# A hybrid decoder block: the FFN's weight sums made by accumulating DMAs, and its first block as eight plain products

## The chip, the cores and the metric

The kernel runs on one core of a Trainium2 chip. The metric is device microseconds of one execution. Profiles come from one profiled execution, and their times count from the first instruction of its span.

## The reference

One decoder block on 512 tokens of width 1024, in float32. Two mixers (a Mamba-2 scan and a gated delta rule) are merged, projected by `w_out` and added to `x`. Behind them stands the part that the change touches, a SwiGLU FFN with 2816 hidden columns:

```python
x = x + merged @ w_out[l]
h = rmsnorm(x, norm_ffn_w[l])
gate, up = jnp.split(h @ w_ffn_in[l], [FFN_HIDDEN], axis=-1)
x = x + (jax.nn.silu(gate) * up) @ w_ffn_down[l]
return rmsnorm(x, final_norm_w)
```

## The kernel before

Every large product is made in three matmuls of a rounded type: each operand is split into a high part (an ACT cast, `whi` for weights) and a low part (a DVE subtraction, `wlo`), and `three` (L322) adds high x high, high x low and low x high in PSUM.

**Order of the work.** The instruction order on TensorE, DVE and ACT is fixed when the program is built. A planner (`Weave`, L34) keeps an estimated clock for each engine; `job`s run one after the other and issue the products, and threads (evictions, norms, sums) are emitted between matmuls by `tick` (L85) when their events are done by that estimate. `until` (L104) moves the planned clock of TensorE on until an event is done. On the chip each engine goes through its own queue in order and waits on semaphores.

**Weights.** `stream` is the list of weight units in the order of use. A unit is 512 rows by 256 columns, 512 KB. `load` (L306) issues the DMA of the next unit on SP's queue, or calls a function that does and returns a tile; `ahead(n_split, n_load)` (L280) splits units ahead of the product in hand, and `ahead(2, 3)` stands in the middle of each product. `whi`, `wlo` and the load tile `wst` have three buffers each. Larger tiles share pools: `b8` (16 buffers), `m4` (5) and, for 512 elements a partition, `s2` (8). PSUM has eight banks (`psum`).

**The FFN input.** Tokens are halved (0 to 255, 256 to 511), and so are the 1024 input columns. With the gate and the up columns of one block of 256 hidden columns, this is a 2 x 2 product of 2 x 2 blocks: activations a11, a12 (first token half), a21, a22 (second), and weights b11, b21 (gate) and b12, b22 (up). Strassen's scheme, in Winograd's form, makes it in seven products instead of eight: P1 = a11 b11, P2 = a12 b21, and five products with sums on one side or on both. There are 11 blocks (`NB`). A product is two column groups of 128 times four row groups times three matmuls of 256 columns: 24 matmuls.

The activation sums are made once, by `h2_sums` (L1141): for token half 0 it splits a11 (P1) and a12 (P2), for half 1 a22 (P4) and then the sums for P5, P7, P6 and P3, each a DVE sum and a split. They wait for the norm and the transposes of the token tiles (`norm_T`, L382), whose two scalar steps run on GpSimd.

The weight sums are made for each block by GpSimd in `ffn_units` (L1247): t1 = b12 - b11, t2 = b22 - t1, b22 - b12 and b21 - t2, four tensor_tensor operations on 128 x 1024 elements. `ffn_post` (L1288) adds the products of a block and applies Silu and the gate, on ACT and DVE. `act_split` (L1364) splits the result for the down projection, which follows (`down_job`, L1377).

Of the kernel before, what the change touches and what calls it, by code (L numbers as in the profile page):

```python
# [8 lines left out]
F32 = mybir.dt.float32  # L9
F32R = mybir.dt.float32r  # L10
# [116 lines left out]
class Queue:  # L127
# [3 lines left out]
    def __getattr__(self, name):  # L131
        f = getattr(self.eng, name)
        wv = self.wv

        def emit(out_, *args, **kw):
            if name == "dma_start":
                wv.cur += 2500.0
                wv.last = None
            else:
                n = free_size(out_)  # L140
                if name == "reciprocal":
                    n *= 8
# [3 lines left out]
                if self.key == "POOL" and name == "tensor_tensor" and ALU.pow not in args:  # L146
                    cost = 200.0 + 2.1 * n
# [31 lines left out]
def hybrid_block_kernel(  # L179
# [21 lines left out]
    def nm(s):  # L201
        uid[0] += 1
        return f"{s}_{uid[0]}"
# [76 lines left out]
    def ahead(n_split, n_load):  # L280

        main = wv.cur
        for i in range(len(splits), min(at[0] + n_split, len(stream))):
            _, a, b = stream[i]
            while len(loads) <= i:
                load()
            wv.cur = max(wv.clock["PE"], loads[i][1])
            hi = wp.tile([P, a, b], F32R, tag="whi", name=nm("whi"))
            lo = wp.tile([P, a, b], F32R, tag="wlo", name=nm("wlo"))
            split(hi, lo, loads[i][0])  # L290
            splits.append((hi, lo, wv.cur))
            if len(loads) < min(i + 1 + n_load, len(stream)):
                load()
        while len(loads) < min(len(splits) + n_load, len(stream)):
            load()
        wv.cur = main

    def fetch(src, a, b, pool=None):
        if pool:
            st = pool([a, b], s="wst")  # L300
        else:
            st = wp.tile([P, a, b], F32, tag="wst", name=nm("wst"))
        sy.dma_start(st, src)
        return st

    def load():  # L306
        src, a, b = stream[len(loads)]
# [833 lines left out]
    def h2_sums(th):  # L1141


        (a11, a12) = mid.hq[0][:, 0], mid.hq[0][:, 1]
        if th == 0:
            yield [("h2", 0), ("h2", 1)]
            h2_split("P1", a11)
            yield HOP
            h2_split("P2", a12)
            return  # L1150
        (a21, a22) = mid.hq[1][:, 0], mid.hq[1][:, 1]
        yield [("h2", 2), ("h2", 3), ("a", "P2")]
        h2_split("P4", a22)
        s1 = m4([4, 256], s="s1")
        ve.tensor_tensor(s1, a21, a22, ALU.add)
        yield HOP
        h2_split("P5", s1)
        yield HOP
        ve.tensor_tensor(a21, a11, a21, ALU.subtract)
        h2_split("P7", a21)  # L1160
        yield HOP
        ve.tensor_tensor(a11, s1, a11, ALU.subtract)
        h2_split("P6", a11)
        yield HOP
        ve.tensor_tensor(a12, a12, a11, ALU.subtract)
        h2_split("P3", a12)

    def wo_job(q):
        if q == 0:
# [77 lines left out]
    def ffn_units(fp, order):  # L1247
        w = Batch()

        def get(r, c, pool=None):  # L1250
            return fetch(ffn_src(r, c, fp), 4, 256, pool)

        def t1():
            w.b11 = get(0, 0)
            w.b12 = get(0, 1, m4)
            w.t1 = b8([4, 256], F32, "t1")
            gp.tensor_tensor(w.t1, w.b12, w.b11, ALU.subtract)

        def t2():
            w.b22 = get(1, 1, m4)  # L1260
            w.t2 = m4([4, 256], s="t2")
            gp.tensor_tensor(w.t2, w.b22, w.t1, ALU.subtract)

        def of(name):
            if name == "P1":
                t1()
                return w.b11
            if name == "P6":
                if not hasattr(w, "t1"):
                    t1()  # L1270
                t2()
                return w.t2
            if name == "P7":
                gp.tensor_tensor(w.b12, w.b22, w.b12, ALU.subtract)
                return w.b12
            if name == "P5":
                w.b21 = get(1, 0)
                return w.t1
            if name == "P2":
                return w.b21  # L1280
            if name == "P4":
                gp.tensor_tensor(w.t2, w.b21, w.t2, ALU.subtract)
                return w.t2
            return w.b22

        return [((lambda n=n: of(n)), 4, 256) for n in order]

    def ffn_post(fp):  # L1288

        v = ffn.act[fp]  # L1290
        lo, hi = slice(0, 256), slice(256, 512)

        def half(s_):
            t = s2([512], s_)
            return t, t.rearrange("p (j t) -> p j t", j=2)

        bk = ffn.banks[fp]
        yield [("P", fp, "P1")]
# [6 lines left out]
        yield [("P", fp, "P7")]  # L1305
        u3, _ = half("u3")
        ve.tensor_tensor(u3, bk["C"], u2, ALU.add)
        yield [("P", fp, "P5")]
        c22, c22v = half("c22")
        ve.tensor_tensor(c22, bk["D"], u3, ALU.add)  # L1310
        finish(("c22", fp))
        yield [("P", fp, "P2")]
        ac.activation(v[:, :, lo], bk["A"].rearrange("p (j t) -> p j t", j=2), AF.Silu)
        yield [("P", fp, "P4")]
        ve.tensor_tensor(u3, bk["E"], u3, ALU.add)
        yield HOP
        ac.activation(v[:, :, hi], u3.rearrange("p (j t) -> p j t", j=2), AF.Silu)
        yield HOP
        ve.tensor_tensor(v[:, :, hi], c22v, v[:, :, hi], ALU.mult)
        yield [("P", fp, "P3")]  # L1320
        ve.tensor_tensor(u2, bk["D"], u2, ALU.add)
        ve.tensor_tensor(v[:, :, lo], u2.rearrange("p (j t) -> p j t", j=2), v[:, :, lo], ALU.mult)
        finish(("ffn", fp))
        yield True

    ffn.banks = {}

    def product(fp, name):

        if fp not in ffn.banks:  # L1330
            ffn.banks[fp] = {}
            if fp % 2 == 0:
                ffn.pair = b8([2, 2, T], F32, "act")
            ffn.act.append(ffn.pair[:, fp % 2])
            spawn(ffn_post(fp))
        until(("a", name), *{"P2": [("p1", fp)], "P3": [("c22", fp)]}.get(name, []))
        bk = ffn.banks[fp]
        fresh = BANK[name] not in bk
        if fresh:
            bk[BANK[name]] = psum("pw")  # L1340
        p = bk[BANK[name]]
        ahi, alo = ffn.a[name]
        whi, wlo = unit()
        for j in range(2):
            cs = slice(j * P, (j + 1) * P)
            for kk in range(4):
                three(p[:, 256 * j:256 * j + 256], (whi[:, kk, cs], wlo[:, kk, cs]), (ahi[:, kk], alo[:, kk]),
                      fresh and j == 0 and kk == 0, j == 1 and kk == 3, skip_group_check=True)
                if kk % 2:
                    tick()  # L1350
            if j == 0:
                ahead(2, 3)
        finish(("P", fp, name))

    def ffn_block(fp, order=ORDER):
        for name in order:
            product(fp, name)

    for fp in range(NB):
        job(lambda fp=fp: ffn_block(fp), *ffn_units(fp, ORDER))  # L1360

    act = {}

    def act_split():  # L1364

        for fp in range(NB):
            yield [("ffn", fp), ("P", NB - 1, "P5" if fp == 0 else ORDER[(fp + 1) // 2 - 1])]
# [118 lines left out]
```

## Time and profile before

| | us |
|---|---|
| median of three runs | 1045.8 (1044.96 to 1046.6) |
| the profiled execution | 1047.84 |
| its span, first to last instruction | 1046.1 |
| TensorE busy in the span | 998.0 |
| DVE, ACT, GpSimd (POOL) busy | 673.6, 457.6, 193.5 |

Matmuls overlap, so TensorE's busy time is longer than its work at full rate: read the starts. In a timeline row the bracket gives the idle time before the operation and who ended it. Line 155 is the helper through which DVE, ACT, GpSimd and SP operations go, line 166 the one of matmuls; go by the tiles' names. The granted clock is a share of TensorE's 2.4 GHz.

### The profile page before, as it was taken

The numbers are of one execution on the slowest core, as the hardware profiler recorded it, in microseconds if no ns is written. First come the engines' busy times: TensorE is split into PE (matmuls) and PEld (weight loads), VectorE is DVE, ScalarE is ACT, GpSimd is POOL, SyncE is SP. The second block draws the span as 40 slices with busy tenths as digits, with TensorE's granted clock in tenths as the row PEclk, the third lists the DMA queues.
The fourth block names the chain that finished last, engine by engine and source line by source line (L and its number), as shares of the span: only waits on it lengthen the run. The fifth ranks groups of instructions, "written<-read, shape, count | busy, mean of one in ns | idle before, by whom it ended". The sixth has DMA issues, their size and how long they took to land.

```text
span 1046.1 us, 15585 instructions
## 1 busy us (share of the span) xinstructions
PE 998.0 (95%) x6370; PEld 885.6 (85%) x6370; DVE 673.6 (64%) x901; ACT 457.6 (44%) x834; POOL 193.5 (18%) x148
## 2 busy tenths in 40 slices
PE   7999999999999999999999999398999999999997
PEld 5888878888888888788998899398999989988886
DVE  5665899545576867842255545578887888772422
ACT  5466445467867472022344323443334443552322
POOL 2041002100101210000011003344545555000000
PEclk9999999999999999999999999789999999999999
DMA  6242232121124533243223531222233322232222
GB/s 191 80 165 61 84 99 81 42 81 42 41 62 141 178 95 96 72 124 96 86 82 101 162 100 61 60 81 81 81 109 116 100 81 82 81 120 90 94 81 81
DMA packets 84072, 98.30 MB, mean 94 GB/s; under 512 B 5738, under 2 KB 75527, under 8 KB 83232
## 3 DMA queue, kind: packets, MB, share of 16 engines
q1 hardware_dynamic: 83998, 97.30, 30.3%
q8 instruction: 50, 0.82, 0.3%
q14 instruction: 22, 0.18, 0.1%
q10 hardware_dynamic: 2, 0.00, 0.0%
HBM read 95.14 MB, written 2.15 MB: 93 GB/s over the span
## 4 chain that ended last, share of the span: by engine, by line
PE 83%; DVE 11%; ACT 2%; issue 2%; SPq 1%; DMA 0%; POOL 0%; POOLq 0%; ACTq 0%; DVEq 0%
PE pw L166 52%; PE pdn L166 11%; PE pt L166 8%; DVE wlo L155 5%; PE pyd L166 1%; DVE act L155 1%; DVE gd L155 1%; PE pm L166 1%; DVE xb L155 1%; PE pt L170 1%; PE pn L170 1%; SPq L155 1%; PE pa L166 1%; PE po L166 1%; PE pg L166 1%
## 5 line engine op out<-in xcount | busy, mean ns | idle before, releaser
L155 DVE TENSOR_TENSOR wlo<-wst,whi 128x1024 fp32r<-128x1024 f32 x158 | 215.1, 1363 | 223.7 <-ACT whi L155 217.2
L155 ACT CAST whi<-wst 128x1024 fp32r<-128x1024 f32 x158 | 165.4, 1049 | 207.1 <-PE pw L166 114.4
L166 PE MATMUL pw<-h2w,whi 128*128 128x256 f32 x1232 | 225.3, 285 | 14.2 <-ACT h2w L155 12.2
L166 PEld LDWEIGHTS pw<-h2w,whi 128*128 128x128 f32 x1232 | 194.1, 194 | 14.7 <-ACT h2w L155 12.4
L166 PE MATMUL pw<-hhi,whi 128*128 128x512 f32 (+1 forms) x496 | 196.7, 397 | 1.4 <-ACT whi L155 1.4
L166 PE MATMUL pw<-hhi,wlo 128*128 128x512 f32 (+1 forms) x496 | 191.1, 385 | 2.3 <-DVE wlo L155 2.3
L166 PE MATMUL pw<-hlo,whi 128*128 128x512 f32 (+1 forms) x496 | 190.6, 384 | 0.0
L166 PE MATMUL pw<-h2w,wlo 128*128 128x256 f32 x616 | 177.2, 288 | 12.1 <-DVE wlo L155 12.1
L166 PEld LDWEIGHTS pw<-h2w,wlo 128*128 128x128 f32 x616 | 119.2, 194 | 15.5 <-DVE wlo L155 15.5
L166 PEld LDWEIGHTS pw<-hhi,wlo 128*128 128x128 f32 x496 | 93.7, 189 | 21.9 <-DVE wlo L155 3.0
L166 PEld LDWEIGHTS pw<-hhi,whi 128*128 128x128 f32 x496 | 93.8, 189 | 17.9 <-ACT whi L155 1.6
L166 PE MATMUL pdn<-whi,actw 128*128 128x512 f32 x352 | 108.4, 389 | 0.0
L166 PEld LDWEIGHTS pw<-hlo,whi 128*128 128x128 f32 x496 | 94.0, 190 | 16.3
L166 PEld LDWEIGHTS pdn<-whi,actw 128*128 128x128 f32 x352 | 66.1, 188 | 13.6
L155 POOL TENSOR_TENSOR t<-wst,t 128x1024 f32<-128x1024 f32 x22 | 61.9, 2814 | 49.7 <-DVE wlo L155 40.1
L166 PE MATMUL pdn<-wlo,actw 128*128 128x512 f32 x176 | 68.5, 389 | 0.0
L155 DVE TENSOR_TENSOR wlo<-t,whi 128x1024 fp32r<-128x1024 f32 x33 | 57.7, 1749 | 3.0 <-ACT whi L155 3.0
L155 POOL TENSOR_TENSOR t<-wst,wst 128x1024 f32<-128x1024 f32 x11 | 29.5, 2678 | 153.7 <-PE pt L166 75.7
L155 DVE SCALAR_TENSOR_TENSOR acc<-pw,pg,acc 128x511 f32<-128x511 f32 (+2 forms) x72 | 53.6, 747 | 2.8 <-ACT acc L155 0.9
L155 ACT CAST whi<-t 128x1024 fp32r<-128x1024 f32 x33 | 34.5, 1045 | 32.4 <-PE pw L166 32.4
L166 PE MATMUL pw<-yg,whi 128*128 128x512 f32 x128 | 42.9, 416 | 0.0
L155 POOL TENSOR_SCALAR ss<-ss 128x1 f32<-128x1 f32 x16 | 4.9, 304 | 196.4 <-ACT jk L155 179.2
(262 smaller groups left out, 1639.6 us busy)
## 6 DMA issues: line engine op xcount, KB each, us to landing
wst<-in_w_in_dram SPq DMA_DIRECT2D x68, 512.0 KB, 3.7
wst<-in_w_ffn_in_dram SPq DMA_DIRECT2D x44, 512.0 KB, 3.8
wst<-in_w_ffn_down_dram SPq DMA_DIRECT2D x22, 512.0 KB, 3.8
decay<-gcd SPq DMA_DIRECT2D x6, 1024.0 KB, 4.9
wst<-in_w_proj_gdn_dram SPq DMA_DIRECT2D x8, 512.0 KB, 3.5
wst<-in_w_proj_ssm_dram SPq DMA_DIRECT2D x8, 512.0 KB, 3.5
wst<-in_w_out_dram SPq DMA_DIRECT2D x8, 512.0 KB, 3.6
xt<-in_x_dram SPq DMA_DIRECT2D x4, 512.0 KB, 4.5
```

The lines of the kernel that those rows point to most:

```text
L155: return f(out_, *args, **kw)
L166: return self.eng.matmul(out_, lhsT, rhs, **kw)
L170: return self.eng.transpose(out_, in_, identity)
```

## The change

The change does four things.

1. The order of the products and the signs of the sums are others (`ORDER`, `BANK`). All weight sums are now additions: x is b11, then b11 + b12, then b11 + b12 + b22; y is b22, then b22 + b12; z is b21, then b21 + x. The two accumulations into x, the one into y and the one into z are DMAs with `accum_op=ALU.add`, issued on GpSimd's queue. Three of them read the weights from DRAM once more, the last reads x from SBUF.
2. A new class, `Source`, holds for a unit what loads it and what is to be done right after its split (`post`, called in `ahead`). So x is added to as soon as P1's split has read it, and the next product that uses x takes its split from the same tile.
3. Block 0 is made as eight plain products (`ffn_first`): the four of the first token half first, then the four of the second. Its four weight units are split once into `b8` tiles that stay (`keep`). `h2_sums` also splits a21 for it.
4. `ffn_post` evicts in another grouping: six DVE evictions and two gate products per block instead of five and two; block 0 has one Silu and one product for each half. The planner's cost for GpSimd's tensor_tensor is dropped.

```diff
@@ in ahead()
+            src = stream[i][0]
+            if getattr(src, "keep", False):
+                both = b8([2, a, b], F32R, "wkeep")
+                hi, lo = both[:, 0], both[:, 1]
+            else:
+                hi = wp.tile([P, a, b], F32R, tag="whi", name=nm("whi"))
+                lo = wp.tile([P, a, b], F32R, tag="wlo", name=nm("wlo"))
             split(hi, lo, loads[i][0])
+            if callable(src):
+                src.post()
@@ in h2_sums()
         yield [("h2", 2), ("h2", 3), ("a", "P2")]
+        h2_split("a21", a21)
+        yield HOP
         h2_split("P4", a22)
         s1 = m4([4, 256], s="s1")
-        ve.tensor_tensor(s1, a21, a22, ALU.add)
+        ve.tensor_tensor(s1, a21, a22, ALU.subtract)
         yield HOP
         h2_split("P5", s1)
-        yield HOP
         ve.tensor_tensor(a21, a11, a21, ALU.subtract)
+        yield HOP
+        ve.tensor_tensor(s1, s1, a11, ALU.subtract)
+        h2_split("P6", s1)
+        yield HOP
+        ve.tensor_tensor(a12, a12, s1, ALU.add)
+        h2_split("P3", a12)
+        yield HOP
         h2_split("P7", a21)
...
-    ORDER = ("P1", "P6", "P7", "P5", "P2", "P4", "P3")
-    BANK = {"P1": "A", "P6": "B", "P7": "C", "P5": "D", "P2": "A", "P4": "E", "P3": "D"}
+    ORDER = ("P1", "P3", "P2", "P5", "P7", "P6", "P4")
+    BANK = {"P1": "A", "P3": "F", "P2": "A", "P5": "D", "P7": "C", "P6": "B", "P4": "E"}
@@ ffn_units()
+        if fp == 0:
+            return [(Source(lambda r=r, c=c: fetch(ffn_src(r, c, 0), 4, 256), keep=True), 4, 256)
+                    for c in range(2) for r in range(2)]
...
+        def get(name, r, c, pool=None):
+            setattr(w, name, fetch(ffn_src(r, c, fp), 4, 256, pool))
+            return getattr(w, name)
+
+        def add(dst, src):
+            gp.dma_start(dst, src, accum_op=ALU.add)
+
+        def t2_t4():
+            add(w.x, ffn_src(1, 1, fp))
+            add(w.z, w.x)
+
+        return [(Source(g, p), 4, 256) for g, p in (
+            (lambda: get("x", 0, 0, m4), lambda: add(w.x, ffn_src(0, 1, fp))),
+            (lambda: get("y", 1, 1, m4), lambda: add(w.y, ffn_src(0, 1, fp))),
+            (lambda: get("z", 1, 0), None),
+            (lambda: w.x, t2_t4),
+            (lambda: w.y, None),
+            (lambda: w.x, None),
+            (lambda: w.z, None))]
@@ ffn_post(), a block that is not the first
+        yield [("P", fp, "P2")]
+        ac.activation(v[:, :, lo], two(bk["A"]), AF.Silu)
         yield [("P", fp, "P6")]
         u2, _ = half("u2")
+        u3, _ = half("u3")
         ve.tensor_tensor(u2, bk["B"], p1, ALU.add)
...
         ve.tensor_tensor(u3, bk["C"], u2, ALU.add)
+        ve.tensor_tensor(u2, bk["F"], u2, ALU.subtract)
+        ve.tensor_tensor(u2, bk["D"], u2, ALU.add)
+        ve.tensor_tensor(v[:, :, lo], two(u2), v[:, :, lo], ALU.mult)
...
+        ve.tensor_tensor(c22, bk["D"], u3, ALU.subtract)
@@ new
+    def ffn_first():
+
+        ffn_start(0)
+        ws = {}
+        for t, cs in ((1, (1, 2)), (2, (2, 1))):
+            for c in cs:
+                p = ffn.banks[0][f"c{t}{c}"] = psum("pw")
+                for r in (1, 2):
+                    name = {(1, 1): "P1", (1, 2): "P2", (2, 1): "a21", (2, 2): "P4"}[t, r]
+                    until(("a", name))
+                    if t == 1:
+                        ws[r, c] = unit()
+                    product(p, ffn.a[name], ws[r, c], r == 1, r == 2, lambda: ahead(2, 3))
+                finish(("P", 0, f"c{t}{c}"))
```

## Rows read from the trace of the kernel before

**Rows 1.** The page's first part: busy time, share of the span, instructions.
```profile
PE 998.0 (95%) x6370; PEld 885.6 (85%) x6370; DVE 673.6 (64%) x901; ACT 457.6 (44%) x834; POOL 193.5 (18%) x148
```

**Rows 2.** TensorE's timeline: an early FFN matmul, and every third of an undisturbed product.
```profile
655.83 0.40 PE L166 MATMUL pw<-h2w,whi 128*128 128x256 f32 x2
...
882.12 0.28 PE L166 MATMUL pw<-h2w,wlo 128*128 128x256 f32 x1
...
882.48 0.28 PE L166 MATMUL pw<-h2w,wlo 128*128 128x256 f32 x1
```

**Rows 3.** Busy time by stretch: length, engines with counts, granted clock, DMA share, GB/s.
```profile
core 0: us, PE busy (x) PEld busy (x) DVE busy (x) ACT busy (x) POOL busy (x), PEclk, DMA share, GB/s
655.80:701.50 45.70, 26.79 (x187) 26.08 (x186) 29.85 (x25) 19.34 (x24) 17.32 (x10) 0.78 0.20 60
730.70:752.57 21.87, 20.66 (x170) 20.26 (x169) 18.77 (x16) 8.84 (x11) 11.42 (x4) 1.00 0.33 97
...
701.50:919.70 218.20, 206.10 (x1683) 202.65 (x1682) 185.77 (x143) 91.89 (x105) 99.47 (x36) 1.00 0.30 92
```

**Rows 4.** TensorE's timeline, its gaps: start, length, operation, count, idle before and releaser.
```profile
639.57 0.39 PE L166 MATMUL pt<-wlo,mgh 128*128 128x256 f32 x1 [1.48 <-DVE wlo L155]
...
663.62 3.48 PE L170 MATMUL pt<-ident,hn 128*128 128x128 f32 x16 [4.75 <-DVE hn L155]
...
679.27 0.58 PE L166 MATMUL pw<-h2w,whi 128*128 128x256 f32 x1 [12.17 <-ACT h2w L155]
681.84 0.58 PE L166 MATMUL pw<-h2w,whi 128*128 128x256 f32 x1 [1.99 <-DVE h2w L155]
...
885.12 0.38 PE L166 MATMUL pw<-h2w,wlo 128*128 128x256 f32 x1 [1.04 <-DVE wlo L155]
```

**Rows 5.** Waits of TensorE, 701.5 to 919.7: total us, times, longest.
```profile
PE pw L166 <- DVE wlo L155: 12.1, 17, 1.5
```

**Rows 6.** The chain of waits in one block: start, length, engine, tile.
```profile
854.32 1.34 DVE act L155
855.66 3.36 DVE wlo L155
859.07 2.91 PE pw L166 x22
861.98 1.21 DVE wlo L155
863.23 11.55 PE pw L166 x94
```

**Rows 7.** Timelines of GpSimd and DVE in one block.
```profile
880.97 2.41 POOL L155 TENSOR_TENSOR t<-wst,t 128x1024 f32<-128x1024 f32 x1 [1.16 <-DVE wlo L155]
...
864.24 0.68 DVE L155 TENSOR_TENSOR u<-pw,p 128x512 f32<-128x512 f32 x1
...
881.53 2.40 DVE L155 TENSOR_TENSOR act<-u,act 128x512 f32<-128x512 f32 x1
```

**Rows 8.** Timelines of ACT and DVE in block 0.
```profile
660.52 1.03 ACT L155 CAST whi<-wst 128x1024 fp32r<-128x1024 f32 x1
...
667.76 1.04 ACT L155 CAST h2w<-hq 128x1024 fp32r<-128x1024 f32 x1
...
668.83 1.23 DVE L155 TENSOR_TENSOR h2w<-hq,h2w 128x1024 fp32r<-128x1024 f32 x1 [3.37 <-ACT h2w L155]
```

**Rows 9.** Timelines of ACT and DVE, one undisturbed split.
```profile
868.93 1.05 ACT L155 CAST whi<-wst 128x1024 fp32r<-128x1024 f32 x1 [1.78 <-PE pw L166]
...
870.01 1.23 DVE L155 TENSOR_TENSOR wlo<-wst,whi 128x1024 fp32r<-128x1024 f32 x1
```

**Rows 10.** DMA issues of the whole span: count, size of each, median us to landing.
```profile
decay<-gcd SPq DMA_DIRECT2D x6, 1024.0 KB, 4.9
wst<-in_w_proj_gdn_dram SPq DMA_DIRECT2D x8, 512.0 KB, 3.5
```

**Rows 11.** The same, 701.5 to 919.7.
```profile
wst<-in_w_ffn_in_dram SPq DMA_DIRECT2D x32, 512.0 KB, 4.2
```

More of the change, by code (lines that the diff above doesn't have):

```diff
@@ L145, in emit @@
                 cost = self.fixed + self.rate * n
-                if self.key == "POOL" and name == "tensor_tensor" and ALU.pow not in args:
-                    cost = 200.0 + 2.1 * n
                 if ALU.pow in args:
@@ L287, in ahead @@
             wv.cur = max(wv.clock["PE"], loads[i][1])
-            hi = wp.tile([P, a, b], F32R, tag="whi", name=nm("whi"))
-            lo = wp.tile([P, a, b], F32R, tag="wlo", name=nm("wlo"))
+            src = stream[i][0]
[5 more added lines that the diff above has]
+                lo = wp.tile([P, a, b], F32R, tag="wlo", name=nm("wlo"))
             split(hi, lo, loads[i][0])
+            if callable(src):
+                src.post()
             splits.append((hi, lo, wv.cur))
@@ L304, in fetch, with __init__, __call__, post @@
         return st
+    class Source:
+        def __init__(self, get, post=None, keep=False):
+            self.get, self.after, self.keep = get, post, keep
+        def __call__(self):
+            return self.get()
+        def post(self):
+            if self.after:
+                main, last = wv.cur, wv.last
+                self.after()
+                wv.cur, wv.last = main, last
     def load():
@@ L1152, in h2_sums @@
         yield [("h2", 2), ("h2", 3), ("a", "P2")]
+        h2_split("a21", a21)
+        yield HOP
         h2_split("P4", a22)
         s1 = m4([4, 256], s="s1")
-        ve.tensor_tensor(s1, a21, a22, ALU.add)
+        ve.tensor_tensor(s1, a21, a22, ALU.subtract)
         yield HOP
         h2_split("P5", s1)
+        ve.tensor_tensor(a21, a11, a21, ALU.subtract)
         yield HOP
-        ve.tensor_tensor(a21, a11, a21, ALU.subtract)
-        h2_split("P7", a21)
-        yield HOP
[L1162 to L1166, printed above, removed]
+        ve.tensor_tensor(s1, s1, a11, ALU.subtract)
[4 more added lines that the diff above has]
+        yield HOP
+        h2_split("P7", a21)
     def wo_job(q):
@@ L1245, in ffn_src, with ffn_units @@
         return w_ffn_in[512 * r:512 * r + 512, off:off + 256].rearrange("(k p) c -> p k c", p=P)
-    def ffn_units(fp, order):
+    def ffn_units(fp):
+        if fp == 0:
+            return [(Source(lambda r=r, c=c: fetch(ffn_src(r, c, 0), 4, 256), keep=True), 4, 256)
+                    for c in range(2) for r in range(2)]
         w = Batch()
[L1250 to L1286, printed above, removed]
+        def get(name, r, c, pool=None):
[14 more added lines that the diff above has]
+            (lambda: w.z, None))]
     def ffn_post(fp):
@@ L1297, in ffn_post, with two @@
         bk = ffn.banks[fp]
+        def two(t):
+            return t.rearrange("p (j t) -> p j t", j=2)
+        if fp == 0:
+            for name, s_ in (("c11", lo), ("c21", hi)):
+                yield [("P", fp, name)]
+                ac.activation(v[:, :, s_], two(bk[name]), AF.Silu)
+                yield [("P", fp, name[:2] + "2")]
+                ve.tensor_tensor(v[:, :, s_], two(bk[name[:2] + "2"]), v[:, :, s_], ALU.mult)
+            finish(("ffn", fp))
+            yield True
+            return
         yield [("P", fp, "P1")]
@@ L1316, in ffn_post @@
         yield HOP
-        ac.activation(v[:, :, hi], u3.rearrange("p (j t) -> p j t", j=2), AF.Silu)
+        ac.activation(v[:, :, hi], two(u3), AF.Silu)
         yield HOP
         ve.tensor_tensor(v[:, :, hi], c22v, v[:, :, hi], ALU.mult)
-        yield [("P", fp, "P3")]
-        ve.tensor_tensor(u2, bk["D"], u2, ALU.add)
-        ve.tensor_tensor(v[:, :, lo], u2.rearrange("p (j t) -> p j t", j=2), v[:, :, lo], ALU.mult)
         finish(("ffn", fp))
@@ L1326, in hybrid_block_kernel, with ffn_start, product @@
     ffn.banks = {}
[L1328 to L1343, printed above, removed]
+    def ffn_start(fp):
+        ffn.banks[fp] = {}
+        if fp % 2 == 0:
+            ffn.pair = b8([2, 2, T], F32, "act")
+        ffn.act.append(ffn.pair[:, fp % 2])
+        spawn(ffn_post(fp))
+    def product(p, a, w, first, last, each=None):
         for j in range(2):
@@ L1346, in product, with ffn_block @@
             for kk in range(4):
-                three(p[:, 256 * j:256 * j + 256], (whi[:, kk, cs], wlo[:, kk, cs]), (ahi[:, kk], alo[:, kk]),
-                      fresh and j == 0 and kk == 0, j == 1 and kk == 3, skip_group_check=True)
+                three(p[:, 256 * j:256 * j + 256], (w[0][:, kk, cs], w[1][:, kk, cs]), (a[0][:, kk], a[1][:, kk]),
+                      first and j == 0 and kk == 0, last and j == 1 and kk == 3, skip_group_check=True)
                 if kk % 2:
                     tick()
[L1351 to L1357, printed above, removed]
+            if j == 0 and each:
+                each()
+    def ffn_first():
[11 more added lines that the diff above has]
+                finish(("P", 0, f"c{t}{c}"))
+    def ffn_block(fp):
+        ffn_start(fp)
+        bk = ffn.banks[fp]
+        for name in ORDER:
+            until(("a", name), *([("p1", fp)] if name == "P2" else []))
+            fresh = BANK[name] not in bk
+            if fresh:
+                bk[BANK[name]] = psum("pw")
+            w = unit()
+            product(bk[BANK[name]], ffn.a[name], w, fresh, True, lambda: ahead(2, 3))
+            finish(("P", fp, name))
     for fp in range(NB):
-        job(lambda fp=fp: ffn_block(fp), *ffn_units(fp, ORDER))
+        job(lambda fp=fp: ffn_block(fp) if fp else ffn_first(), *ffn_units(fp))
     act = {}
@@ L1366, in act_split @@
         for fp in range(NB):
-            yield [("ffn", fp), ("P", NB - 1, "P5" if fp == 0 else ORDER[(fp + 1) // 2 - 1])]
+            yield [("ffn", fp), ("P", NB - 1, ORDER[max(0, (fp + 1) // 2 - 1)])]
             w = b8([2, 2, T], F32R, "actw")
```

7 lines of the change are left out of this document (removed).

## The prediction

> **What bounds the kernel now.** I read the page's first part, then the chain of waits, then TensorE's timeline for its gaps, then the window table by stage. TensorE is busy for 998.0 of 1046.1 us [rows 1], so only its gaps and its work count. The change touches nothing before the first weight sums, made late in the output projection, and the FFN input, which starts at 655.83 [rows 2]. At the other end the chain runs from 919.70 through the down projection, on TensorE alone.
>
> The FFN input has two parts. Block 0 runs from 655.8 to 701.5, and there TensorE is busy for 26.79 of 45.70 us at a mean granted clock of 0.78 [rows 3]. Its gaps are 4.75 us before the transposes of the last two token tiles, 12.17 us until the ACT half of an activation sum is there, and 1.99 us until the DVE half is [rows 4]. P1 is the only product that can run on the first half of the tokens; P6 needs the whole chain of sums. From 701.5 to 919.7 come blocks 1 to 10. A product is 24 matmuls, and three of them take 0.36 us (882.12 to 882.48) [rows 2], so a product takes 2.88 us and seven take 20.16. The 1680 matmuls of ten blocks would take 201.6 us, and the window took 218.2: 21.82 per block. One block alone takes 21.87, with DVE busy for 18.77 and POOL for 11.42 [rows 3]. TensorE waits 17 times for `wlo` of DVE, 12.1 us of idle time [rows 5], 1.04 of them before 885.12 [rows 4]; the rest of the 16.6 us is the first matmul after each wait, which starts without the usual overlap.
>
> Why is `wlo` late? In the chain [rows 6] one `wlo` takes 3.36 us and the next 1.21, at one size. The slow ones lie beside GpSimd: its sum runs from 880.97 for 2.41 us while a DVE product runs from 881.53 for 2.40 [rows 7]. The two hold each other up, and twice per block a split comes too late for TensorE.
>
> **The change, part by part.**
>
> *GpSimd's sums go.* About 3.6 tensor_tensor per block leave (36 with 99.47 us in the window [rows 3]); none is a term by itself, but DVE's slow operations should fall to their short form. DVE's load per block becomes 7 splits at 1.21 [rows 6], six evictions at 0.68 (one more than now) and two products at no more than the slow 2.40 [rows 7]: 17.4 us at most, under 20.16. The F bank eviction is hidden by that room; without it, it would cost 0.68 per block. ACT's work stays (8.84 of 21.87 [rows 3]). The same sums made for block 0 during the output projection held `wlo` until 639.57, idle 1.48 us [rows 4]: with the first matmul after it, **-1.6 us**.
>
> *Block 0 as eight products.* It adds one product, 2.88 us, in exchange for order: four products need only the first token half. From 655.83 they take 11.5 us; within them lie the 16 transposes, 3.48 us as they ran [rows 4], mostly waiting for `hn`: to 670.9. Their weights: the third unit's cast ran at 660.52 [rows 8], its split so ends near 662.8, 1 us after it is wanted (655.83 + 5.76 + 0.24 = 661.8), which lies inside the waiting part of the 3.48. The first split of the second half (a22 before, a21 now) was cast at 667.76 and subtracted from 668.83 for 1.23 [rows 8]: ready at 670.1. Now two more weight casts of 1.05 may stand ahead of it in ACT's queue: 672. So TensorE waits 1 us, and the other four products end at 672 + 11.5 = 683.5, against 701.5: **-18.0 us**. The activation sums begin near 672 beside those four products: 3.5 us each for cast, subtraction and one sum as long as the subtraction [rows 8], in the order P5, P6, P3, P7, with one more sum of 1.2 us ahead of P6. P3 is done near 672 + 3 x 3.5 + 1.2 = 683.7, and wanted at 686.4; weight splits come between, so it is about due. I take 0 and keep 3 us above. The half-speed clock goes with the gap, and is inside the 18. On POOL the two norm steps of token tile 3 now stand before the first accumulating DMA, not behind a 2.4 us sum [rows 7]; the planner could also put them behind a waiting DMA, which costs a few us once.
>
> *Accumulating DMAs.* Per block SP issues three loads, not four; GpSimd issues four accumulations: x += b12 after P1's split, y += b12 after P3's, x += b22 after P5's, and z += x when that has landed. Let D be the time from the end of a split to the landing. A cast starts when the product three places before frees its buffer (868.93, idle until TensorE [rows 9]); cast and subtraction take 2.3 us together (868.93 to 871.24). Count from a block's start:
> - P5's cast starts at 2.88 + 0.2 and its split ends at 5.4; x lands at 5.4 + D, z at 5.4 + 2D; P4's split ends at 7.7 + 2D; `wlo` is wanted 0.24 after the product's start. P4 is the seventh product and adds 2.88: the block takes 10.3 + 2D, if that is over 20.16.
> - There is also a loop through three accumulations. P4's cast stands before the next block's P1 cast in ACT's queue, so P1's split ends 3.5 us after P4's cast starts; x += b12 takes D, P5's split 2.3, then 2D: 5.8 + 3D. It passes 20.16 from D = 4.8.
>
> Behind a waiting P4 cast on ACT stand the next casts and a Silu; behind its split on DVE the evictions, for which only the banks wait, and eight banks cover over a block.
>
> No accumulating DMA and no DMA of GpSimd's is in the trace. Below, the nearest rows are plain loads of the same 512 KB: 3.5 us alone [rows 10], 4.2 in this stretch [rows 11]. Above, reading both operands as two plain loads in series: 8.4. Between them stands one row with as many bytes as both operands together, the 1024 KB `decay` load at 4.9 [rows 10]. I take 4.9 because that is the row nearest in bytes: a period of 20.5, so 10 x (21.82 - 20.5) = **-13.2 us**. At 4.8 or less it is -16.6; at 8.4 a block takes 31.0, +92.
>
> The Trainium skill, "DMA: Bandwidth & Descriptors" (Anatomy of one DMA), fits a GpSimd-issued DMA as 2.0 us plus bytes at 436 GB/s; no run shows it yet, and an estimate by it is 3.2 us here, so no block would stall. Against that, "Collectives: The Full Stack" (The bandwidth ceiling) says that a DMA that adds reads two sources on one ring and so moves at half the rate. By rows that is a rival: one load is 0.33 x 21.87 / 4 = 1.8 us of all 16 engines [rows 3], so D = 3.5 + 1.8 = 5.3, the period 21.7, and the blocks gain 1.2 us.
>
> *Sum.* 1.6 + 18.0 + 13.2 = 32.8 us. The profiled execution took 1047.84 us (span 1046.1 and 1.7 around it), 0.2% above the median of 1045.8; 1047.84 - 32.8 = 1015.0, and from the median **1013**.
>
> **Rivals.**
> 1. *Half rate (D 5.2 to 5.9).* For: the second read; the 97 GB/s at a DMA share of 0.33 [rows 3] become 11 engine-times of 1.8 us = 19.8 of 20.16 us, so transfers queue. Against: if the second read lies beside the first. At 5.3: 1045.8 - 18.0 - 1.6 - 1.2 = 1025; up to 1043 at 5.9.
> 2. *Slower: the chain of accumulations becomes the loop's bound.* A GpSimd operation beside a DVE one holds it and is held, 2.41 and 2.40 us [rows 7], and DVE stays busy for most of a block. If GpSimd's issue of a DMA is held in the same way, by about 2 us, D = 6.9, the period is 26.5, the blocks cost +47 and the kernel ends at 1073. It decides from 5.8 + 3D = 21.82 + 1.96, D = 6.0. Against: an issue reads no weight tile on GpSimd, and DVE at 17.4 of 20.16 us leaves gaps. The Trainium skill, "SBUF — State Buffer" (SBUF: two separate sides), says that DVE can keep GpSimd from writing descriptors, in a mode that no row here names.
> 3. *Block 0 doesn't gain.* If buffers or the sums come late and TensorE stands still for 10 us at the low clock, the first term is 6: 1025.
>
> **How the numbers follow.** My forecast with D up to 5.2, no stall included: 0.55. Rival 1: 0.21. Rival 2: 0.16. Rival 3: 0.08. A measurement of this kernel tells 0.2% (2 us) from no change. Faster takes the forecast, rivals 1 and 3 but for a strip at D near 6: 0.81; within 0.2%: 0.03; slower: 0.16. Low end: no stall and block 0 at its best, 1045.8 - 16.6 - 1.6 - 20 = 1007. High end: rival 1's end and the first strip of rival 2, 1045; what is left is most of rival 2. The forecast's own range is 1007 to 1022.
>
> **What would show it.** Right: no GpSimd tensor_tensor in the FFN; `wlo` at 1.2 us throughout; block 0 at about 28 us with the clock near 1; TensorE's gaps in blocks 1 to 10 gone or waiting for P4's cast; accumulations landing in about 5 us. Wrong: TensorE waiting 2 us or more per block on a `whi` that waits for a DMA (D too small here), a gap over 5 us in block 0, or `wlo` still at 2.4 to 3.4 us.

## The result, and the profile after

The kernel after took 1055.55 us (median of four runs, 1055.14 to 1057.0) against 1046.2 before, a ratio of 1.0094 [1.0076, 1.0111]: slower by 0.9%, where 1013 had been forecast. The profiled execution took 1055.14 us, 7.3 more than the one before.

The page's first part, its queues and its DMA issues of the kernel after (issues: KB each, median us from issue to landing):

```profile
PE 1008.9 (96%) x6394; PEld 890.8 (85%) x6394; DVE 611.3 (58%) x904; ACT 453.9 (43%) x831; POOL 118.0 (11%) x144
...
q1 hardware_dynamic: 78718, 92.06, 28.3%
q0 software_dynamic: 17280, 20.97, 12.7%
...
L153 DVE TENSOR_TENSOR wlo<-wst,whi 128x1024 fp32r<-128x1024 f32 x184 | 225.7, 1236 | 297.1 <-ACT whi L153 290.9
...
wst<-in_w_ffn_in_dram POOLq DMA_DIRECT2D x30, 512.0 KB, 5.9
...
wst<-wst POOLq DMA_DIRECT2D x10, 512.0 KB, 4.6
```

Against [rows 1], GpSimd's busy time fell from 193.5 to 118.0 us, and DVE's from 673.6 to 611.3. In the FFN every `wlo` now takes about 1.24 us; those of 3.36 [rows 6] are gone. So the contention that the change could remove is removed. What came in is an accumulating DMA of 5.9 us.

TensorE's rows in block 0 up to the start of block 1, the counterpart of [rows 4]:

```profile
654.91 6.46 PE L164 MATMUL pw<-h2w,wkeep 128*128 128x256 f32 x50
662.00 2.18 PE L164 MATMUL pw<-h2w,wkeep 128*128 128x256 f32 x16 [0.64 <-DVE wkeep L153]
664.02 1.91 PE L168 MATMUL pt<-ident,hn 128*128 128x128 f32 x16
665.69 15.35 PE L164 MATMUL pw<-h2w,wkeep 128*128 128x256 f32 x126
680.88 0.40 PE L164 MATMUL pw<-h2w,whi 128*128 128x256 f32 x2
```

The sixteen transposes stand in one piece, the gaps of 4.75, 12.17 and 1.99 us are gone, and block 1 begins at 680.88 where it began at 701.5. Block 0 takes 25.97 us (654.91 to 680.88) instead of 45.7, and with what stands ahead of it the gain is 20.6 us.

The stretches of the two parts and one block in them (columns: window, length, busy time of PE, PEld, DVE, ACT and POOL, granted clock, DMA share, GB/s), to be read against [rows 3]:

```profile
655.80:680.60 24.80, 24.11 (x200) 23.71 (x200) 18.70 (x19) 14.74 (x20) 4.26 (x6) 1.00 0.62 150
680.60:926.50 245.90, 217.94 (x1685) 208.58 (x1684) 138.31 (x150) 94.30 (x108) 44.97 (x38) 0.98 0.70 140
...
723.77:748.13 24.36, 21.72 (x172) 20.70 (x172) 13.56 (x15) 8.74 (x10) 4.75 (x4) 1.00 0.76 151
```

The down projection starts at 926.5, so ten blocks took 245.6 us, 24.56 each against 21.82: +27.4. With -20.6 that is +6.8 of the 7.3. The whole loss lies in the ten Strassen blocks, and no engine is full there: in one block of 24.36 us TensorE is busy for 21.72 and DVE for 13.56. Nor is it the clock, which was granted in full (1.00) in that block.

What TensorE waits for in that stretch (columns: us in total, times, longest), the counterpart of [rows 5]:

```profile
PE pw L164 <- DVE wlo L153: 16.7, 26, 0.8
PE pw L164 <- ACT whi L153: 11.2, 16, 2.0
```

The new row is the second: a weight's high part that is late. Who makes it late shows in one block on ACT, on DVE and on GpSimd (bracket: idle time before, and who ended it). ACT first:

```profile
723.77 2.94 ACT L153 CAST whi<-wst 128x1024 fp32r<-128x1024 f32 x3 [3.51 <-DMA wst<-wst]
728.94 1.05 ACT L153 CAST whi<-wst 128x1024 fp32r<-128x1024 f32 x1 [2.22 <-PE pw L164]
731.94 0.59 ACT L153 COPY p<-pw 128x512 f32<-128x512 f32 x1 [1.95 <-PE pw L164]
734.22 0.63 ACT L153 ACTIVATE act<-u 128x512 f32<-128x512 f32 x1 [1.70 <-DVE u L153]
734.76 1.03 ACT L153 CAST whi<-wst 128x1024 fp32r<-128x1024 f32 x1
738.77 1.05 ACT L153 CAST whi<-wst 128x1024 fp32r<-128x1024 f32 x1 [2.98 <-DMA wst<-in_w_ffn_in_dram]
739.73 0.59 ACT L153 ACTIVATE act<-pw 128x512 f32<-128x512 f32 x1
743.28 1.05 ACT L153 CAST whi<-wst 128x1024 fp32r<-128x1024 f32 x1 [2.96 <-DMA wst<-in_w_ffn_in_dram]
748.13 1.04 ACT L153 CAST whi<-wst 128x1024 fp32r<-128x1024 f32 x1 [3.81 <-DMA wst<-wst]
```

DVE in the same stretch:

```profile
724.85 2.36 DVE L153 TENSOR_TENSOR wlo<-wst,whi 128x1024 fp32r<-128x1024 f32 x2 [3.33 <-ACT whi L153]
727.13 0.69 DVE L153 TENSOR_TENSOR u<-pw,p 128x512 f32<-128x512 f32 x1
727.85 2.14 DVE L153 TENSOR_TENSOR u<-pw,u 128x512 f32<-128x512 f32 x3
730.03 0.69 DVE L153 TENSOR_TENSOR act<-u,act 128x512 f32<-128x512 f32 x1
730.64 0.68 DVE L153 TENSOR_TENSOR c<-pw,u 128x512 f32<-128x512 f32 x1
731.24 2.35 DVE L153 TENSOR_TENSOR wlo<-wst,whi 128x1024 fp32r<-128x1024 f32 x2
733.50 0.68 DVE L153 TENSOR_TENSOR u<-pw,u 128x512 f32<-128x512 f32 x1
...
735.82 1.23 DVE L153 TENSOR_TENSOR wlo<-wst,whi 128x1024 fp32r<-128x1024 f32 x1 [0.24 <-ACT whi L153]
```

And GpSimd, whose four rows are the issues of x += b12, y += b12, x += b22 and z += x:

```profile
727.51 1.30 POOL L153 DMA_DIRECT2D wst<-in_w_ffn_in_dram  x1 [7.48 <-DVE wlo L153]
732.75 1.28 POOL L153 DMA_DIRECT2D wst<-in_w_ffn_in_dram  x1 [3.94 <-DVE wlo L153]
737.34 1.28 POOL L153 DMA_DIRECT2D wst<-in_w_ffn_in_dram  x1 [3.31 <-DVE wlo L153]
743.49 0.89 POOL L153 DMA_DIRECT2D wst<-wst  x1 [4.86 <-DMA wst<-in_w_ffn_in_dram]
```

Read them as a loop (a dash marks a product of the next block, as P5'):

- The row x3 at 723.77 begins with P4's cast, which waited for z += x. Its split starts on DVE at 724.85, and from there DVE goes without a pause to 734.2: the splits of P4 and P1', the six operations of evictions and gate that had gathered behind P4's split, the splits of P3' and P2', and the last eviction.
- That eviction lets the last Silu go on ACT (734.22), and behind the Silu stands P5's cast (734.76). From P4's cast to P5's cast: 1.08 + 9.37 + 0.54 = 11.0 us.
- P5's cast and split take 2.3, x += b22 is issued at 737.34 and lands for P6's cast at 743.28; z += x is issued at 743.49 and lands for the next P4 cast at 748.13.

The casts released by z += x come at 699.20, 723.77, 748.13 and so on to 920.20, nine periods of 24.56 us. From the end of P5's split (737.05) to the cast that its accumulation releases, D2, it is 6.2 us here and 6.4 in the mean of the nine periods; from there to the next P4 cast, D3, 4.85 here and 4.9 in the mean. The loop is 11.0 + 2.3 + D2 + D3 = 13.3 + 11.3 = 24.6 us. The terms follow one another, so their sum must be the period; what the rows add is who holds each of them.

The first accumulation (x += b12) isn't in this loop: issued at 727.51 and landed 5.9 us later, at 733.4, it is there 1.3 us before P5's cast at 734.76. So the queues are the longer of two ways to P5's cast, by 1.3 us only.

### The profile page after: what moved, and what is told of

The parts are those of the page before. It is cut to its first block, busy times and chain, and to the rows that moved or that the text cites. A ratio compares the mean times of both kernels' runs of the same rounds, so it can differ in the third digit from the quotient of the medians.

```text
span 1053.4 us, 15628 instructions
## 1 busy us (share of the span) xinstructions
PE 1008.9 (96%) x6394; PEld 890.8 (85%) x6394; DVE 611.3 (58%) x904; ACT 453.9 (43%) x831; POOL 118.0 (11%) x144
## 3 DMA queue, kind: packets, MB, share of 16 engines
q0 software_dynamic: 17280, 20.97, 12.7%
## 5 line engine op out<-in xcount | busy, mean ns | idle before, releaser
L153 DVE TENSOR_TENSOR wlo<-wst,whi 128x1024 fp32r<-128x1024 f32 x184 | 225.7, 1236 | 297.1 <-ACT whi L153 290.9
L153 ACT CAST whi<-wst 128x1024 fp32r<-128x1024 f32 x184 | 190.9, 1048 | 285.5 <-PE pw L164 101.0
L164 PE MATMUL pw<-h2w,whi 128*128 128x256 f32 x1120 | 209.1, 288 | 11.2 <-ACT whi L153 11.2
L164 PEld LDWEIGHTS pw<-h2w,whi 128*128 128x128 f32 x1120 | 177.4, 195 | 14.9 <-ACT whi L153 14.9
L164 PE MATMUL pw<-h2w,wlo 128*128 128x256 f32 x560 | 163.3, 292 | 16.7 <-DVE wlo L153 16.7
L153 POOL DMA_DIRECT2D wst<-in_w_ffn_in_dram x30 | 38.9, 1295 | 158.5 <-DVE wlo L153 154.7
L164 PEld LDWEIGHTS pdn<-wlo,actw 128*128 128x128 f32 x176 | 33.2, 188 | 6.7
L164 PE MATMUL pt<-whi,hhi 128*128 128x256 f32 x128 | 36.5, 285 | 0.0
L164 PE MATMUL pt<-wlo,mgh 128*128 128x256 f32 x128 | 36.3, 284 | 0.1
L164 PE MATMUL pt<-whi,mgh 128*128 128x256 f32 x128 | 36.4, 284 | 0.0
```

The source lines that it names most:

```text
L164: return self.eng.matmul(out_, lhsT, rhs, **kw)
```

## The experiments

Two theories at first. L: the ten blocks lose by a loop of dependent steps through the accumulations; at first this was the prediction's loop with three landings. E: the accumulations fill the 16 DMA engines, and the transfers queue. Later runs divided L's loop into its terms. The numbers stand against the kernel before on the same chip (1045.4 to 1047.3).

**The two parts alone.** `r_first`: block 0 as eight products, the old order with GpSimd's sums elsewhere.

```diff
-    ORDER = ("P1", "P3", "P2", "P5", "P7", "P6", "P4")
+    ORDER = ("P1", "P6", "P7", "P5", "P2", "P4", "P3")
...   (units of blocks 1 to 10 and their sums as in the kernel before)
```

> Only block 0 is changed (eight plain products, a21 split for it); blocks 1 to 10 keep GpSimd's sums, the old order and the old signs. Theory L (the change loses in blocks 1 to 10 because a loop through three accumulating DMAs in series is longer than seven products) expects the gain of block 0 alone: block 0 ends about 21 us earlier and the blocks stay at 21.8 us, 1046.2 - 21 = 1025. Theory E (the DMA engines' added work is what costs) expects the same here. A theory that block 0 gives nothing of its own expects 1046.

Measured: 1038.2, ratio 0.9925 [0.9908, 0.9942], 13 us less gain than expected. GpSimd's timeline in block 0 says why:

```profile
661.81 3.51 POOL L155 TENSOR_TENSOR t<-wst,wst 128x1024 f32<-128x1024 f32 x1 [4.95 <-DMA wst<-in_w_ffn_in_dram]
665.40 3.24 POOL L155 TENSOR_TENSOR t<-wst,t 128x1024 f32<-128x1024 f32 x1
668.72 0.51 POOL L155 TENSOR_SCALAR ss<-ss 128x1 f32<-128x1 f32 x1
669.31 2.74 POOL L155 TENSOR_TENSOR wst<-wst,wst 128x1024 f32<-128x1024 f32 x1
672.01 1.53 POOL L155 TENSOR_TENSOR ss<-ss,mhalf 128x1 f32<-128x1 f32 x1
```

Two of block 1's sums stand ahead of the two norm steps (`ss`) of the last token tile and a third between them, and on TensorE the last transposes wait:

```profile
676.54 1.94 PE L170 MATMUL pt<-ident,hn 128*128 128x128 f32 x8 [5.99 <-DVE hn L155]
```

To test that, `r_first1` leaves those sums out:

```diff
-            gp.tensor_tensor(w.t1, w.b12, w.b11, ALU.subtract)
+            if fp > 1:
+                gp.tensor_tensor(w.t1, w.b12, w.b11, ALU.subtract)
...   (the other three sums likewise)
```

> r_first (eight plain products, then GpSimd's sums) with the sums of block 1 left out, so GpSimd and its shared time with DVE are free while block 0 runs. If these sums are why r_first gained 8 us and not 21: 13 us more, 1024 to 1026, and no gap over 1 us in block 0. If block 0's gain is held by something else: 1036.

Measured: 1027.59 (one run), no gap over 0.63 us in block 0. Block 1 starts at 681.40 us there and at 694.23 in `r_first`: 12.8 of the 13 us that `r_first` lacked. The two parts of the change aren't independent: block 0 gains in full only when GpSimd's sums are gone.

`r_accum`: accumulating DMAs in all eleven blocks, no plain block.

```diff
-        if fp == 0:
-            return [(Source(..., keep=True), 4, 256) ...]
-        job(lambda fp=fp: ffn_block(fp) if fp else ffn_first(), *ffn_units(fp))
+        job(lambda fp=fp: ffn_block(fp), *ffn_units(fp))
```

> The other part alone: accumulating DMAs in all eleven blocks, no plain block, a21 not split. L and E both expect the loss without block 0's gain: 1055.5 + 21 + 3 (block 0 now also has the loop, 24.4 for 20.2) = 1076 to 1080. If the two parts were not independent it would come out more than 5 us away from that.

Measured: 1075.95, ratio 1.0288 [1.027, 1.0306], as expected: this half of the change costs by itself about 30 us. It doesn't tell L from E, which expected the same.

**Is it the loop?** `x_noz` leaves out the last accumulation.

```diff
             add(w.x, ffn_src(1, 1, fp))
-            add(w.z, w.x)
```

> The changed kernel without z += x: P4 takes b21 alone as its weights, so part of the computation is left out. L: the loop goes from 24.4 to 19.6 us, under the 20.16 of seven products, 1055.5 - 42 = 1013. E: 9/11, also 1013. If the chain of two accumulations still stalls at P6: 1020 to 1030.

Measured: 1024.09, ratio 0.9789 [0.9774, 0.9803]; a block takes 21.6 us. So 1013 was missed by both theories; the third expectation, a stall at P6, came true. About 3 of D3's 4.9 us are gained, not all: P6's cast, released by x += b22, now begins the row x3, and from it to P5's cast it is 12.9 us (801.23 to 814.17), again through the queues behind the Silu; with 2.3 and 6.3 that is the period, 21.5. The loop has a second branch, 3 us shorter:

```profile
801.23 2.94 ACT L153 CAST whi<-wst 128x1024 fp32r<-128x1024 f32 x3 [2.98 <-DMA wst<-in_w_ffn_in_dram]
...
813.63 0.63 ACT L153 ACTIVATE act<-u 128x512 f32<-128x512 f32 x1 [0.75 <-DVE u L153]
814.17 1.03 ACT L153 CAST whi<-wst 128x1024 fp32r<-128x1024 f32 x1
```

`x_dvez` makes z + x on DVE ahead of P4's split instead, `x_dvez2` the same sum ahead of P6's split.

```diff
+            ve.tensor_tensor(w.z, w.z, w.x, ALU.add)   # ahead of P4's split; in x_dvez2 ahead of P6's
-            add(w.z, w.x)
```

> The changed kernel, but z += x is a DVE sum (1.2 us) right ahead of P4's split instead of a fourth accumulating DMA. L: the loop loses 4.8 us of landing and gains 1.2: 24.4 - 3.6 = 20.8 us per block, total 1055.5 - 36 = 1020. E: engine work falls from 3 + 4 x 2 to 3 + 3 x 2 units, 9/11 of 24.4 = 20.0, so TensorE's 20.16 binds: 1013. A theory that GpSimd's issue or DVE's load is at fault (D): DVE gets 1.2 us more per block, so no gain or slower.

> As x_dvez (z += x on DVE), but the sum stands ahead of P6's split instead of P4's, so it doesn't wait behind P6's wlo in DVE's queue and P4's cast follows P6's at once. x_dvez had 23.1 us per block. L, with the queues' order as part of the loop: 2.2 us less, 20.9 per block, 1020. E (6 + 3 units of engine work as in x_dvez): no change from x_dvez, 1041.

Measured: 1040.78, ratio 0.9949 [0.9934, 0.9964], and 1024.87, ratio 0.9794 [0.9777, 0.9812]. In the first the sum stands in DVE's queue behind P6's split, which waits for x: a 1.2 us sum in place of a 4.6 us DMA, yet 23.1 us a block and 20 us more in all than L had expected. Put one place earlier in the queue, it gains 16 us more, as much as leaving the sum out (`x_noz`). The place in an engine's queue counts here, not the price.

`c_two` keeps the two accumulations that are off the loop; b22 is loaded by SP, and both sums of the loop are on DVE.

```diff
-            add(w.x, ffn_src(1, 1, fp))
-            add(w.z, w.x)
+            ve.tensor_tensor(w.x, w.x, w.u, ALU.add)   # ahead of P6's split
+            ve.tensor_tensor(w.z, w.z, w.x, ALU.add)
...
-            (lambda: w.x, t2_t4),
+            (lambda: (get("u", 1, 1), w.x)[1], None),
```

> A candidate: only the two first accumulating DMAs stay (x += b12, y += b12). b22 is loaded once more by SP, and x += b22 and z += x are DVE sums ahead of P6's split (2.4 us of DVE per block, about 16.5 of 20.2 in all). L: the loop holds one landing of 6 us instead of three, so TensorE's 20.16 us binds, up to 0.5 us above it: 1055.5 - 40 = 1015. E: engine work 4 + 2 x 2 = 8 units instead of 11, 17.8 us, also not bound: 1013. A theory that DVE cannot carry the sums: 1030 or more.

Measured: 1013.51, ratio 0.968 [0.9662, 0.9697], the fastest of all. Its page and one window:

```profile
PE 994.9 (98%) x6394; PEld 884.9 (87%) x6394; DVE 635.0 (63%) x924; ACT 455.3 (45%) x831; POOL 94.9 (9%) x124
```

```profile
720.00:890.00 170.00, 168.80 (x1371) 166.21 (x1370) 135.70 (x146) 77.64 (x87) 19.26 (x15) 1.00 0.63 140
```

TensorE is busy for 168.80 of 170 us at full clock. The two accumulations that are left land after 6.4 us, no sooner than before, and P7's cast still waits about 3 us a block for one of them. But only that one landing stands between one block's P7 cast and the next, the loop stays under seven products, and TensorE doesn't notice.

`c_dve` goes on: all four sums on DVE, all loads by SP.

```diff
-            gp.dma_start(dst, src, accum_op=ALU.add)
+            ve.tensor_tensor(dst, dst, src, ALU.add)
...   (SP loads b12 into a tile of its own; y += b12 moves behind P5's split, between x += b22 and z += x)
```

> No accumulating DMA at all: the four weight blocks are loaded by SP as in the kernel before, and all four sums are DVE operations of 1.2 us. DVE's load per block is then 8.5 + 4.1 + 1.4 + 4.9 = 18.9 of 20.16 us. If TensorE still binds: 1013, as the candidate with two accumulations. If DVE's queue order at 94% makes splits late: 1 to 2 us per block, 1023 to 1033.

Measured: 1020.85, ratio 0.9756 [0.9737, 0.9774]: DVE is busy for 139.94 of 160 us, and TensorE waits for `wlo` nine times, 6.8 us in all. The wait comes once a block, for P7's split, ahead of which three sums stand in DVE's queue (772.11 to 775.74 in one block). So two sums each is the better of the two kernels; four on DVE in other places of its queue weren't tried.

**Is it the engines?** `x_load` adds one plain 512 KB load per block.

```diff
-            (lambda: get("z", 1, 0), None),
+            (lambda: (get("u", 1, 0), get("z", 1, 0))[1], None),
```

> The changed kernel with one more plain 512 KB load per block (b21 a second time, into a tile that nothing reads). It adds engine work but stands in no chain. E: 12 units instead of 11, 26.6 us per block, 1055.5 + 22 = 1077. L: landings get a little longer by collisions, 0 to 1 us per block, 1055 to 1065.

Measured: 1056.74 (one run). The DMA share rose to 0.81 and the landing stayed at 6.0: E, which expected 1077, is rejected as a bound by the sum of bytes.

`x_plain` makes the same four DMAs as copies, `x_quarter` accumulates only a quarter of each.

```diff
-            gp.dma_start(dst, src, accum_op=ALU.add)
+            gp.dma_start(dst, src)                                          # x_plain
+            gp.dma_start(dst[:, 0:1], src[:, 0:1], accum_op=ALU.add)        # x_quarter
```

> The changed kernel with the four DMAs of GpSimd as plain copies of the same bytes: the weights are overwritten instead of summed, so the sums are left out. It measures what the adding costs: if each needs the second read, landing falls from 5.9 to about 4.1 us (one engine time of 1.8 less) and the loop from 24.4 to 24.4 - 3 x 1.8 = 19.0, under 20.16: 1013. If GpSimd's issue and the fixed part make the 5.9, it stays near 1050.

> The changed kernel with each accumulating DMA cut to a quarter of its rows (128 KB), so three quarters of the weight sums are left out. It separates the fixed part of a landing from the part that goes with bytes. If bytes at two reads each cost 2 x 1.8 us, the landing falls from 5.9 by 0.75 x (3.6 + 1.0 of issue) to about 2.5 us, the loop to 11.0 + 2.3 + 2 x 2.5 = 18.3, and 20.16 binds: 1013. If the fixed part rules (over 4.5 us), the loop stays over 22: 1031 or more.

Measured: 1024.14 and 1011.28 (one run each). The queue and the issues of `x_plain`:

```profile
q0 software_dynamic: 5760, 20.97, 6.2%
...
wst<-in_w_ffn_in_dram POOLq DMA_DIRECT2D x30, 512.0 KB, 4.2
wst<-wst POOLq DMA_DIRECT2D x10, 512.0 KB, 3.6
```

At the same 20.97 MB a copy takes half the engine time of an accumulation (6.2% against 12.7%) and lands after 4.2 and 3.6 us, close to the 4.1 expected. The time expected, 1013, counted three landings in the loop and was missed by 11 us. The way from P4's cast to P5's stays at 11.0 us and P5's split at 2.3, while D2 and D3 fall to 4.6 and 3.8 in the mean of nine periods: 13.3 + 8.4 = 21.7, the period. So it is the landings alone that make the difference of 2.9 us to the kernel after. At a quarter of the bytes the landing is 3.2 and 3.0, the loop (13.3 + 6.6 = 19.9 by the medians) falls just below the 20.16 us of seven products, and TensorE is busy for 159.16 of 160 us.

**The 11.0 us.** `x_silu` emits the last eviction and its Silu one product later, so that P5's cast no longer stands behind them.

```diff
-        yield [("P", fp, "P4")]
+        yield [("P", fp, "P4")] + ([("P", fp + 1, "P3")] if fp < NB - 1 else [])
```

> The changed kernel, but the eviction of P4 and the Silu behind it are emitted after the next block's P3, so behind the next P5's cast in ACT's queue. Theory S (revised): the loop of 24.4 us goes from P4's cast through TensorE's P4, its eviction, its Silu to P5's cast, 11.0 us in all the traces so far, then P5's split 2.3 and the landings 6.2 and 4.8; the first accumulation (landed 1.3 us earlier) is not in it. With the Silu out of the way P5's cast waits for that landing, 9.7 us after P4's cast: 23.1 per block, 1055.5 - 13 = 1042. Theory L as predicted (three landings in the loop, no Silu): no change, 1055. If the later eviction brings a wait of its own: 1055 or slower.

Measured: 1051.73, ratio 1.0049 [1.0031, 1.0067], little more than a quarter of the gain. On ACT, P4's cast and the P5 cast behind it:

```profile
796.42 2.95 ACT L153 CAST whi<-wst 128x1024 fp32r<-128x1024 f32 x3 [3.82 <-DMA wst<-wst]
...
806.11 1.05 ACT L153 CAST whi<-wst 128x1024 fp32r<-128x1024 f32 x1 [0.93 <-DMA wst<-in_w_ffn_in_dram]
```

P5's cast comes 9.7 us after P4's here and 10.1 in the mean of nine periods, instead of 11.0, so the queue did hold it; now it waits for x += b12, which has only then landed. But the period fell only to 24.39, because D2 and D3 grew from 6.4 and 4.9 to 6.7 and 5.3 in the mean (single landings up to 7.5 and 6.0 us from the issue). y += b12 and x += b22 are now issued 3.8 us apart in the mean instead of 4.6. Why the landings grew isn't settled by this run.

**Which accumulations are in the loop?** `x_nod1` leaves out x += b12, `x_noy` leaves out y += b12.

```diff
-            (lambda: get("x", 0, 0, m4), lambda: add(w.x, ffn_src(0, 1, fp))),
+            (lambda: get("x", 0, 0, m4), None),          # x_nod1; the same for "y" in x_noy
```

> The changed kernel without x += b12, so P5, P6 and P4 lack b12: part of the computation is left out. By the loop as predicted (three landings and the splits) a whole landing of 6 us leaves it and TensorE's 20.16 binds: 1013. By the loop read from the traces since (P4's cast, TensorE's P4, its eviction and Silu, P5's cast, two landings: 11.0 + 2.3 + 6.3 + 4.8) the first accumulation is not in it: 24.4 per block, 1055; at most 1 us per block less, if the other landings get shorter because fewer transfers run beside them.

> The changed kernel without y += b12, so P7 lacks b12. It stands beside x += b22 on the queue and in no chain of the loop by either theory. Both: 24.4 per block, 1055, unless it lengthens the landing of x += b22: then D2 falls from 6.3 to 5 or so and the time to about 1042. In the kernel with the Silu moved, a shorter wait ahead of P5's cast came with a landing of up to 7.6 us, which this would explain.

Measured: 1053.09 and 1067.75 (one run each). Without x += b12 the period is 24.56, as in the kernel after: the prediction's loop, in which that landing was the first of three, isn't the one that binds. Without y += b12 the kernel is 12 us slower, which neither theory had: the period is 26.0. GpSimd's timeline of `x_noy`:

```profile
808.06 1.30 POOL L153 DMA_DIRECT2D wst<-in_w_ffn_in_dram  x1 [7.45 <-DVE wlo L153]
817.89 1.28 POOL L153 DMA_DIRECT2D wst<-in_w_ffn_in_dram  x1 [8.54 <-DVE wlo L153]
825.88 0.89 POOL L153 DMA_DIRECT2D wst<-wst  x1 [6.71 <-DMA wst<-in_w_ffn_in_dram]
```

SP's queue in the same stretch has this load, 0.9 us behind the issue of x += b22:

```profile
818.76 0.37 SPq L153 DMA_DIRECT2D wst<-in_w_ffn_in_dram  x1
```

The DMA engines from the issue of x += b22 to its landing, here and in the kernel after (columns as in the windows above; the last is GB/s):

```profile
819.00:825.60 6.60, 5.60 (x47) 5.39 (x45) 0.00 (x0) 0.47 (x1) 0.17 (x1) 1.00 0.85 159
738.70:743.20 4.50, 4.50 (x40) 4.50 (x39) 1.23 (x1) 1.55 (x2) 0.00 (x0) 1.00 0.95 159
```

P7's cast no longer waits for a DMA, so P7's split follows P5's at once and the next load is issued at once. It runs beside x += b22, and P6's cast, which needs x, comes only at 825.68, 7.8 us after the issue instead of 5.9. In the kernel after, the load comes 3.8 us behind the issue (741.11 and 737.34). Both stretches move 159 GB/s; but 6.60 us of it are 1.05 MB, both transfers to the end, and 4.50 us are 0.72 MB, x += b22 and the beginning of the load. So the longer landing goes with the place of one transfer, and didn't come with a higher mean share in `x_load`; that the load is its cause is read from these rows and wasn't tried by itself.

## Why the prediction was wrong

The step that failed is the loop of the accumulating DMAs: its path and the size of its landings. The other two parts came close.

- **GpSimd's sums go** (mechanism right): `wlo` at 1.24 us throughout the FFN, POOL's tensor_tensor gone. The 1.6 us ahead of block 0 can't be told: the FFN input starts at 654.91 instead of 655.83, and in the other runs between 652.96 and 655.42.
- **Block 0** (right in mechanism and size): 18.0 us forecast, 19.7 measured (45.67 to 25.97 us). The wait for the split of the third unit is there at 0.64 us; the clock was 1.00 as expected. That P1 was "the only product that can run on the first half of the tokens" is wrong, P2 = a12 b21 needs no more; it came fifth in the old order. The prediction saw that the norm steps no longer stand behind a sum of GpSimd's, but gave that no price: where they stand behind the sums, in `r_first`, block 1 starts 12.8 us later than in `r_first1`.
- **Accumulating DMAs** (wrong): forecast -13.2 us by a loop of "5.8 + 3D" at D = 4.9, measured +27.4. Two errors make up the 40.6 us.
  - *The loop's path.* The prediction let P5's cast follow P4's by P1's split and one landing, and dismissed the queue: "for which only the banks wait". It isn't only the banks that wait: the late P4 split holds up six DVE operations, these hold the next splits and the last eviction, that one the Silu, and the Silu P5's cast. 11.0 + 2.3 + 2D = 13.3 + 2D took the place of 5.8 + 3D.
  - *The size of D.* From the end of a split to the landing of an accumulation from DRAM it is 6.2 to 6.4 us instead of 4.9; only the one from SBUF is as forecast, 4.9 from the cast that the landing before it releases.
  - How the 40.6 us are shared depends on the order. With the path put right first, the loop at the predicted D is 23.1 us instead of 20.5, 26 us in ten blocks, and the landings add 15. With the landings put right first, the predicted loop is 5.8 + 6.2 + 6.4 + 4.9 = 23.3 us, 28 us, and the path adds 13. Either error alone would have left the kernel faster than before, at an estimate of 1038 to 1040 us by these sums; it took both to make it slower.
- **Rival 2** named the right thing, the chain of accumulations as the bound, by a price that isn't there: GpSimd's issue took 1.28 to 1.30 us and its DMA landed after 5.9 whether DVE worked beside it (727.51, 732.75) or not (737.34), so it isn't held. The hold of descriptor writing that the Trainium skill, "SBUF — State Buffer" (SBUF: two separate sides), tells of is for one mode of DVE; beside the operations that DVE runs here the trace shows none.
- **Rival 1**, half rate, had a cause of the larger D right: the adding makes the landings 5.9 instead of 4.2 us and 4.6 instead of 3.6 (`x_plain`), and the kernel 1055.55 instead of 1024.14. Its sum was too low all the same, 21.7 us a block at D = 5.3, where the loop as it is gives 23.9. The Trainium skill, "Collectives: The Full Stack" (The bandwidth ceiling), lets a DMA that adds move at half the rate, for its two reads; the trace agrees in the mean of the forty, 12.7% against 6.2% of the engines for 20.97 MB. But the packets differ too (last section), so that the second read is what costs isn't shown. The Trainium skill, "DMA: Bandwidth & Descriptors" (Anatomy of one DMA), gave an estimate of 3.2 us, with which no block would have stalled; measured are 4.2 for the plain copy from DRAM and 5.9 for the accumulation.

That `c_two` ends at the 1013 us of the forecast is luck: it is another kernel, without the loop that the forecast had mis-sized.

## What to carry to other kernels

When an operation is replaced by a DMA with a longer latency, write down the loop with every instruction that stands between two of its steps in the same engines' queues, not only those that depend on one another: here 9.9 of 24.6 us went by in the queues of DVE and ACT, and the dependent way beside them was only 1.3 us shorter, so shortening the one brings up the other (`x_silu`, `x_noz`). An accumulating DMA outside the loop cost nothing (x += b12, in `x_nod1`), and without the other one the blocks even became longer (`x_noy`); of the 4.9 us of one inside it 3 came back when it was left out (`x_noz`). Choose by that which sums go where, as `c_two` does with two on each side. And two parts of a change need not add up: run each alone before adding their gains.

## What the runs showed of the hardware

- An accumulating DMA of 512 KB took 5.9 us from DRAM and 4.6 from SBUF to its landing, a plain one on the same queue 4.2 and 3.6, an accumulating one of 128 KB 3.2 and 3.0 (`after`, `x_plain`, `x_quarter`). Its issue holds GpSimd for 1.28 to 1.30 us (0.89 from SBUF), that of the plain copy for 0.75 (0.55).
- Forty of them had three times as many packets as the copies (17280 against 5760) and twice the engine time at the same counted bytes. All the additional packets belong to those from DRAM: thirty alone have 15840 (`x_noz`), 528 each of about 1 KB; that leaves 144 each for the ten from SBUF, as many as a copy has. An estimate from the queue's shares (10.5% of the span in `x_noz`, 12.7% and 6.2% in the other two) is 3.6 us of all 16 engines for one from DRAM, 2.6 for one from SBUF and 1.6 for a copy. How much of that is the second read and how much the smaller packets isn't shown.
- GpSimd's sum of 128 x 1024 took 2.33 to 3.51 us in block 0 of `r_first`, and what stands behind it on GpSimd, two operations on 128 x 1 elements, cost TensorE 5.99 us.
